# A decoder pair with 32 experts on one core: the order of the experts from sums on TensorE, two experts in fixed order, first loads held, no GpSimd splits in block 2

## The chip, the cores and the metric

The kernel runs on one core of a Trainium2 chip. The time is the device time of one execution in microseconds (us). The engines are TensorE (PE, with its weight loads as PEld), VectorE (DVE), ScalarE (ACT), GpSimd (POOL) and SyncE (SP), which here only issues DMAs and loads registers.

## The reference, cut to what matters

The reference puts two transformer blocks behind one another. The first has two kinds of attention and then a mixture of experts: each token takes 4 of 32 experts by its router logits, and each expert is a pair of float32 matrix products with a gated activation between them. The second block has two more kinds of attention, gates and a plain feed-forward layer. All is float32.

```python
top_val, top_idx = lax.top_k(logits, TOP_K)            # 4 of 32 per token
gates = jax.nn.softmax(top_val, axis=-1)
group_sizes = jnp.bincount(flat_e, length=N_EXPERTS)
hgu = lax.ragged_dot(xs, w_gate_up, group_sizes) + b_gate_up[e_sorted]
act = _clamped_swiglu(hgu)
out = lax.ragged_dot(act, w_down, group_sizes) + b_down[e_sorted]
```

Only the 512 tokens of the sequence reach the output. On the inputs of the reference their 2048 choices fall on the 32 experts as 36, 49, 102, 58, 125, 33, 51, 66, 8, 19, 48, 62, 45, 86, 85, 91, 93, 74, 14, 47, 51, 102, 112, 18, 159, 86, 49, 55, 60, 89, 39, 36 (its routing worked out in float32).

## The kernel before, in words

**Numbers.** A float32 operand is held as two float32r parts, high and low, and a product is three matmuls (high by high and the two cross terms: `mm3`, L364 to L367). So each weight chunk (128 x 2048 values, 1 MB) that SP loads into a raw buffer is split: ACT writes the high part (L192), DVE subtracts it and writes the low part (L194; GpSimd does so for the chunks in `st.on_pool`). There are 7 raw buffers in the expert stage (3, 2 and 2 in three pools, later 8) and 3 pairs of split ones (later 4).

**The stream of chunks.** `Stream` holds all weights of the kernel in the order of their use. `dma()` (L147) issues loads while a raw buffer is free and the number stays below `st.limit`; `split()` splits ahead while a split buffer is free and then calls `dma()`; `get()` hands PE the next chunk and frees the one before; `release()` frees one.

**Experts.** Each expert has 12 chunks in three parts of four: gate (part 0), up (1) and down (2), run in the order (v,0), (v-1,2), (v,1). An expert's tokens are gathered from DRAM by an indirect DMA into `xg` (`rows`, L1414), transposed on PE (`turn_x`), and after the down part scattered with addition (`out`, L1499). A tile of 128 rows ("big") does 12 matmuls per chunk; a tile of 64 rows ("small") puts the high and low part side by side and does 8.

**The order.** The first `FIRST` = 4 experts run in fixed order with big tiles. The other 28 are ranked by the number of their tokens: ranks 0 to 12 get big tiles, rank 0 a small tile more, ranks 13 to 27 small ones. `RANKS` gives the order in which the ranks run: 13, 0, 14, 15, and then big and small by turns. Tokens that don't fit go to overflow tiles, of which rank 0's second is the first; only if there is more than one, a loop behind the experts runs (`n_ov > 1`).

**The routing.** The tables of the first four experts (`table`, `table_out`: the rows to gather, their gates) are made before the expert stage. The rest is the generator `routing()`, of which one step runs after each chunk (`aside`): counts on PE, then on DVE the ranks by comparing all 32 x 32 pairs on all 128 partitions, the order, the overflow bases, each token's rank and slot, the one-hot tiles `rv` (on GpSimd) and `soh`, the table of the other experts on PE, and the experts of the overflow tiles. From the expert `FIRST` on, a load takes its expert's number from a register that SP loads from `ordi`.

**The start of the expert stage** (L1556 on): gather the first rows, release two split buffers (so two splits, each followed by a load on SP), transpose the rows, and then chunk by chunk.

**Block 2.** Its chunks are in the same stream. Those of the q and k projections and the next three, and two of the feed-forward layer, are in `st.on_pool`: 17 splits of the low part on GpSimd. GpSimd also does the power -0.5 of the norms (L362) and the rotations of one attention (L1770 to L1772).

Of the kernel before, what the change touches and what calls it, by code (L numbers as in the profile page):

```python
# [9 lines left out]
F32 = mybir.dt.float32  # L10
# [10 lines left out]
P = 128  # L21
# [18 lines left out]
ALPHA = 2.0 ** 0.25  # L40
NEG = -1e30
# [54 lines left out]
class Stream:  # L96
# [48 lines left out]
    def dma(self, n=1 << 30):  # L145
        while self.n_dma < n:
            key = self._raw_key()  # L147
            if key is None:
                return
            j = self.n_dma  # L150
            a, b = self.shape[j]
            pool, bufs = self.raw_pools[key]
            t = pool.tile([P, CH], F32, tag="raw", bufs=bufs, name="raw")
            s = self.src[j]
            if callable(s):
                s = s()
            d = t[:, :a * b].rearrange("p (a b) -> p a b", a=a)
            if isinstance(s, list):
                w = b // len(s)
                for i, x in enumerate(s):  # L160
                    self.nc.sync.dma_start(out=d[:, :, i * w:(i + 1) * w], in_=x)
            elif j in self.halves:
                for i in range(2):
                    self.nc.sync.dma_start(out=d[:, i * a // 2:(i + 1) * a // 2], in_=s[:, i * a // 2:(i + 1) * a // 2])
# [59 lines left out]
def tile_kernel(ctx: ExitStack, tc: tile.TileContext, a, out, cst):  # L224
# [15 lines left out]
    def bank(name="b"):  # L240
        return ps[0].tile([P, 512], F32, tag="b", bufs=3, name=name)
# [985 lines left out]
    e_ = ExitStack()  # L1227
    pe = open_pool(e_, "pe")
    st.open_raw(3, pe, NRAW)
    st.dma()  # L1230

    def routing():

        def full(name, tag, shape, dtype=BF16):
            return rt.tile([P, *shape], dtype, tag=tag, bufs=1, name=name)

        def down(x, n):
            return x.unsqueeze(2).to_broadcast([P, NE, n])
# [6 lines left out]
        b = bank("cnt")[:, :NE]  # L1245
        for j in range(NT):
            nc.tensor.matmul(b, oneb, asg[:, j], start=j == 0, stop=j == NT - 1)
        ei = iota[:, :NE]
        cnt, key, rank, small_, first = (rt.tile([P, NE], F32, name=n) for n in ("cnt", "key", "rank", "small_", "first"))
        nc.vector.tensor_copy(out=cnt, in_=b)  # L1250

        stt(out=key, in0=cnt, scalar=float(NE), in1=ei, op0=ALU.mult, op1=ALU.subtract)
        ts(out=key[:, :FIRST], in0=ei[:, :FIRST], scalar1=-1.0, scalar2=-BIG, op0=ALU.mult, op1=ALU.add)
        yield
        before = full("before", "A", [NE, NE])
        tt(out=before, in0=across(key, NE), in1=down(key, NE), op=ALU.is_gt)
        red(out=rank, in_=before, axis=AX.X, op=ALU.add)
        yield

        who = full("who", "B", [NE, NE])  # L1260
        order = rt.tile([P, NE], F32, name="order")
        tt(out=who, in0=down(ei, NE), in1=across(rank, NE), op=ALU.is_equal)
        with exact():
            tt(out=who, in0=who, in1=across(ei, NE), op=ALU.mult)
        red(out=order, in_=who, axis=AX.X, op=ALU.add)
        nc.vector.tensor_copy(out=ordi, in_=order[0:1])
        ts(out=sel[:, FIRST:], in0=order, scalar1=pm, scalar2=None, op0=ALU.is_equal)
        yield

        nov, over, base = (rt.tile([P, NE], F32, name=n) for n in ("nov", "over", "base"))  # L1270
        ts(out=first, in0=rank, scalar1=0.0, scalar2=None, op0=ALU.is_equal)
        ts(out=small_, in0=rank, scalar1=float(NB), scalar2=None, op0=ALU.is_ge)
        stt(out=small_, in0=rank, scalar=float(NE - FIRST), in1=small_, op0=ALU.is_lt, op1=ALU.mult)

        stt(out=over, in0=small_, scalar=64.0, in1=cnt, op0=ALU.mult, op1=ALU.add)
        stt(out=over, in0=first, scalar=-64.0, in1=over, op0=ALU.mult, op1=ALU.add)
        nc.vector.tensor_copy(out=nov, in_=first)
        for k in range(4):
            stt(out=nov, in0=over, scalar=129.0 + 128 * k, in1=nov, op0=ALU.is_ge, op1=ALU.add)
        yield  # L1280
        with exact():
            tt(out=before, in0=before, in1=across(nov, NE), op=ALU.mult)
        red(out=base, in_=before, axis=AX.X, op=ALU.add)
# [53 lines left out]
        i_ = iota[:, :NOV].unsqueeze(2).to_broadcast([P, NOV, NE])
        m1, m2 = full("m1", "A", [NOV, NE]), full("m2", "B", [NOV, NE])
        end = rt.tile([P, NE], F32, name="end")
        tt(out=end, in0=base, in1=nov, op=ALU.add)  # L1340
        tt(out=m1, in0=i_, in1=across(base, NOV), op=ALU.is_ge)
        tt(out=m2, in0=i_, in1=across(end, NOV), op=ALU.is_lt)
        yield
        with exact():
            tt(out=m1, in0=m1, in1=m2, op=ALU.mult)
            tt(out=m1, in0=m1, in1=across(ei, NOV), op=ALU.mult)
        red(out=eidf, in_=m1, axis=AX.X, op=ALU.add)
# [219 lines left out]
    hrs, gb2 = [], []

# [580 lines left out]
```

## Time and profile before

| | |
|---|---|
| median of 3 runs | 2328.29 us (2325.48 to 2330.32) |
| the profiled execution | 2326.43 us, its span 2324.3 us |
| mean granted clock of TensorE | 0.969 |
| expert stage in the trace | about 331 to 1496 us |
| block 2 in the trace | about 1499 to 2324 us |

The profile is of one execution. An engine's busy time is what its instructions took; matmuls are pipelined, so 10.0 of 10 us busy means that PE always had one under way. An idle time is put down to the instruction that released the engine.

### The profile page before, as it was taken

How to read it: one execution, taken by the hardware profiler on the slowest of the kernel's cores; microseconds unless marked ns; L12 is line 12 of the kernel's file. 1: busy time of each engine (PE TensorE's matmuls, PEld its weight loads, DVE VectorE, ACT ScalarE, POOL GpSimd, SP SyncE). 2: the span in 40 equal slices, each digit the busy share in tenths (PEclk: the TensorE clock that was granted, in tenths of full speed). 3: DMA queues.
4: the chain of work that ended last, by engine and by line, in shares of the span. 5: the costliest groups of instructions: out<-in, count | busy, mean ns of one | idle time of the engine just before them, and what ended most of it. 6: DMA issues, size and time to landing. Idle time of an engine off the chain costs nothing. (4 is left out here: it accounts for less than half of the span.)

```text
span 2324.3 us, 27360 instructions
## 1 busy us (share of the span) xinstructions
PE 2184.6 (94%) x10215; PEld 1724.1 (74%) x10215; DVE 1660.4 (71%) x1820; ACT 1311.2 (56%) x1407; POOL 400.0 (17%) x299
## 2 busy tenths in 40 slices
PE   7889967999999999999999999789999999999998
PEld 6677855776777777777777777567887888888886
DVE  5875569987598999999999999755565346343435
ACT  3463444776597888888888888534455222232230
POOL 4200031101021101123321232031352003000000
PEclk9999978999999999999999999899999999999999
DMA  6212166998799999999999999742122333222220
GB/s 225 83 49 91 52 224 197 359 355 308 242 367 348 406 394 396 395 396 389 389 391 395 391 391 387 271 120 59 51 73 73 102 134 107 92 92 91 82 100 37
DMA packets 193817, 529.08 MB, mean 228 GB/s; under 512 B 17777, under 2 KB 64761, under 8 KB 193681
## 3 DMA queue, kind: packets, MB, share of 16 engines
q1 hardware_dynamic: 183632, 503.16, 58.5%
q0 software_dynamic: 8320, 19.94, 3.3%
q10 hardware_dynamic: 1728, 4.20, 0.5%
q8 instruction: 82, 1.34, 0.2%
q14 instruction: 55, 0.44, 0.1%
HBM read 510.97 MB, written 25.71 MB: 231 GB/s over the span
## 5 line engine op out<-in xcount | busy, mean ns | idle before, releaser
L194 DVE TENSOR_TENSOR wlo<-raw,whi 128x2048 fp32r<-128x2048 f32 (+2 forms) x439 | 999.8, 2303 | 189.8 <-ACT whi L192 188.8
L192 ACT ACTIVATE whi<-raw 128x2048 fp32r<-128x2048 f32 (+2 forms) x460 | 867.7, 1898 | 348.6 <-PE bk L367 146.2
L1499 POOL DMA_INDIRECT sums_d<-ob,gidx x33 | 96.7, 2932 | 851.2 <-ACT ob L1498 844.8
L366 PE MATMUL gu<-wlo,x 128*128 128x512 f32 x544 | 217.4, 400 | 8.7 <-DVE wlo L194 8.7
L365 PE MATMUL gu<-whi,x 128*128 128x512 f32 x544 | 222.4, 409 | 0.0
L1468 PE MATMUL gu<-wlo,x 128*128 128x512 f32 x512 | 211.2, 412 | 6.1 <-DVE x L371 3.0
L367 PE MATMUL gu<-whi,x 128*128 128x512 f32 x544 | 216.8, 399 | 0.0
L1469 PE MATMUL gu<-whi,x 128*128 128x512 f32 x512 | 204.1, 399 | 0.0
L365 PE MATMUL bk<-xT,wlo 128*128 128x512 f32 (+2 forms) x464 | 187.0, 403 | 0.6 <-ACT xT L370 0.3
L366 PE MATMUL bk<-xT,whi 128*128 128x512 f32 (+2 forms) x464 | 183.1, 395 | 2.1 <-DVE xT L371 2.1
L367 PE MATMUL bk<-xT,whi 128*128 128x512 f32 (+2 forms) x464 | 183.0, 394 | 0.0
L365 PEld LDWEIGHTS gu<-whi,x 128*128 128x128 f32 x544 | 104.3, 192 | 36.3 <-issue 11.4
L366 PEld LDWEIGHTS gu<-wlo,x 128*128 128x128 f32 x544 | 104.1, 191 | 33.3 <-DVE wlo L194 11.3
L1414 POOL DMA_INDIRECT xg<-h_d,gidx x33 | 114.5, 3468 | 77.4 <-PE trx L380 67.6
L194 POOL TENSOR_TENSOR wlo<-raw,whi 128x2048 fp32r<-128x2048 f32 (+2 forms) x21 | 82.6, 3937 | 236.8 <-ACT whi L192 223.1
L367 PEld LDWEIGHTS gu<-whi,x 128*128 128x128 f32 x544 | 103.9, 191 | 23.9
L1468 PEld LDWEIGHTS gu<-wlo,x 128*128 128x128 f32 x512 | 97.9, 191 | 29.4 <-DVE x L371 3.1
L1468 PE MATMUL dn<-wlo,at 128*128 128x512 f32 x256 | 106.7, 417 | 9.7 <-DVE at L371 3.7
L2056 DVE SCALAR_TENSOR_TENSOR xr<-xr,bk 128x512 f32<-128x512 f32 (+1 forms) x42 | 27.8, 661 | 121.4 <-PE bk L367 121.3
L1469 PEld LDWEIGHTS gu<-whi,x 128*128 128x128 f32 x512 | 97.9, 191 | 19.8
L365 PE MATMUL dn<-whi,at 128*128 128x512 f32 x272 | 110.3, 406 | 0.0
L367 PE MATMUL dn<-whi,at 128*128 128x512 f32 x272 | 108.6, 399 | 0.0
(484 smaller groups left out, 4281.4 us busy)
## 6 DMA issues: line engine op xcount, KB each, us to landing
raw<-in_w_gate_up_dram SPq DMA_DIRECT2D x256, 1024.0 KB, 15.7
raw<-in_w_down_dram SPq DMA_DIRECT2D x128, 1024.0 KB, 15.5
raw<-in_w_ff_dram SPq DMA_DIRECT2D x32, 1024.0 KB, 5.6
raw<-in_w_in_dram SPq DMA_DIRECT2D x14, 1024.0 KB, 5.3
raw<-in_w_in_dram SPq DMA_DIRECT2D x24, 256.0 KB, 3.4
raw<-in_w_o_dram SPq DMA_DIRECT2D x4, 1024.0 KB, 5.1
raw<-in_w_in_dram SPq DMA_DIRECT2D x8, 512.0 KB, 7.3
raw<-in_w_out_dram SPq DMA_DIRECT2D x4, 1024.0 KB, 5.0
```

The source lines that it names most:

```text
L192: nc.scalar.activation(out=hi[:, sl], in_=t[:, sl], func=AF.Copy)
L194: eng.tensor_tensor(out=lo[:, sl], in0=t[:, sl], in1=hi[:, sl].bitcast(F32), op=ALU.subtract)
L365: nc.tensor.matmul(o, ll, rh, start=start, stop=False)
L366: nc.tensor.matmul(o, lh, rl, start=False, stop=False)
L367: nc.tensor.matmul(o, lh, rh, start=False, stop=stop)
L1414: nc.gpsimd.indirect_dma_start(out=xg[:self.n], out_offset=None, in_=h1_d, in_offset=bass.IndirectOffsetOnAxis(ap=self.gi[:self.n], axis=0 ...
L1468: nc.tensor.matmul(o, x[0][:, kk], wl[:, k, sl], start=kk == 0, stop=False)
L1469: nc.tensor.matmul(o, x[0][:, kk], wh[:, k, sl], start=False, stop=False)
L1499: nc.gpsimd.indirect_dma_start(out=sums_d, out_offset=bass.IndirectOffsetOnAxis(ap=self.gi[:self.n], axis=0), in_=ob[:self.n], in_offset=N ...
L2056: nc.vector.scalar_tensor_tensor(out=r, in0=r, scalar=ALPHA if first else 1.0, in1=acc[:, sl], op0=ALU.mult, op1=ALU.add)
```

## The change

The routing computes each expert's rank on its own partition (32 partitions, the other 32 experts along the row), and turns what must stand on all partitions into sums over partitions by small matmuls with ones: the order and the ranks in one, the overflow bases in two, the experts of the overflow tiles in one. The one-hot tile `oh` is bfloat16. `FIRST` is 2: two experts run in fixed order, 30 are ranked, and the ranks run as 13, 0, 14, 15, 16, 17, and then big and small by turns, so there are two big tiles fewer and two small ones more. No load is issued from before the first gather until the order stands: the first two steps of the routing run between the two releases and before the first transposes, and then the free raw buffers are filled by loads on ACT's queue. The gather of the third tile waits for the table. No chunk of block 2 is split on GpSimd.

```diff
-FIRST = 4
+FIRST = 2
...
-RANKS = [NB, 0, NB + 1, NB + 2] + [r for i in range(NB - 1) for r in (1 + i, NB + 3 + i)]
-RANKS += list(range(2 * NB + 2, NE - FIRST))
+RANKS = [NB, 0] + list(range(NB + 1, NE - FIRST - NB + 1)) + [r for i in range(NB - 1) for r in (1 + i, NE - FIRST - NB + 1 + i)]
...
-                self.nc.sync.dma_start(out=d, in_=s)
+                self.queue.dma_start(out=d, in_=s)
...
-    st.on_pool.update(range(n2, len(st.src) + 3))
...
-    st.on_pool.update((len(st.src), len(st.src) + 1))
...
-    oh = rt.tile([P, 16, NE], F32, name="oh")
+    oh = rt.tile([P, 16, NE], BF16, name="oh")
...
     st.open_raw(3, pe, NRAW)
-    st.dma()
...
+            nc.tensor.matmul(b[:NE, :NE], oneb[:, :NE], asg[:, j], start=j == 0, stop=j == NT - 1)
+        for j in range(NT):
+            nc.tensor.matmul(b[:NE, NE:NE + 2], asg[:, j], oneb[:, :2], start=j == 0, stop=j == NT - 1)
+        nc.vector.tensor_copy(out=cn, in_=b[:NE, :NE + 2])
+        stt(out=key, in0=cn[:, :NE], scalar=float(NE), in1=ei, op0=ALU.mult, op1=ALU.subtract)
+        ts(out=key[:, :FIRST], in0=ei[:, :FIRST], scalar1=-1.0, scalar2=-BIG, op0=ALU.mult, op1=ALU.add)
+        stt(out=keyp, in0=cntp, scalar=float(NE), in1=me, op0=ALU.mult, op1=ALU.subtract)
+        ts(out=keyp[:FIRST], in0=me[:FIRST], scalar1=-1.0, scalar2=-BIG, op0=ALU.mult, op1=ALU.add)
+        ts(out=mw[:, 0], in0=key, scalar1=keyp, scalar2=None, op0=ALU.is_lt)
+        red(out=rankp_, in_=mw[:, 0], axis=AX.X, op=ALU.add)
+        ts(out=rankp_, in0=rankp_, scalar1=-1.0, scalar2=float(NE - 1), op0=ALU.mult, op1=ALU.add)
+        ts(out=mw[:, 1], in0=ei, scalar1=rankp_, scalar2=me, op0=ALU.is_equal, op1=ALU.mult)
+        nc.tensor.matmul(b[:, :2 * NE], all_, mw.rearrange("p u e -> p (u e)"), start=True, stop=True)
         yield
-        tt(out=before, in0=across(key, NE), in1=down(key, NE), op=ALU.is_gt)
-        red(out=rank, in_=before, axis=AX.X, op=ALU.add)
...
-        tt(out=who, in0=down(ei, NE), in1=across(rank, NE), op=ALU.is_equal)
-            tt(out=who, in0=who, in1=across(ei, NE), op=ALU.mult)
-        red(out=order, in_=who, axis=AX.X, op=ALU.add)
...
+        nc.vector.tensor_copy(out=ordi, in_=b[0:1, NE:2 * NE])
+        ts(out=sel[:, FIRST:], in0=b[:, NE:2 * NE], scalar1=pm, scalar2=None, op0=ALU.is_equal)
+        nc.vector.tensor_copy(out=rows[:, 0], in_=b[:, :NE])
...
+        ts(out=novs[:, :NE], in0=mw[:, 0], scalar1=nov, scalar2=None, op0=ALU.mult)
+        nc.vector.tensor_copy(out=novs[:, NE:], in_=nov.to_broadcast([NE, 2]))
         yield
-            tt(out=before, in0=before, in1=across(nov, NE), op=ALU.mult)
-        red(out=base, in_=before, axis=AX.X, op=ALU.add)
...
+        nc.tensor.matmul(b[:, :NE + 2], all_, novs, start=True, stop=True)
+        nc.tensor.matmul(b[:NE, NE + 2:NE + 4], mw[:, 0], novs[:, NE:], start=True, stop=True)
         yield
+        nc.vector.tensor_copy(out=rows[:, 1], in_=b[:, :NE])
+        nc.vector.tensor_copy(out=eidi[:, NOV:], in_=b[:, NE:NE + 1])
+        nc.vector.tensor_copy(out=basec, in_=b[:NE, NE + 2:NE + 3])
...
         table_out(tb, NC, FIRST)
+        ranked.append(True)
+        next_gather()
         yield
...
+        nc.tensor.matmul(b, all_, m1, start=True, stop=True)
+        yield
+        nc.vector.tensor_copy(out=eidf, in_=b)
...
+    st.limit = st.n_dma
     next_gather()
+    more = routing()
     st.release()
+    next(more)
     st.release()
+    next(more)
     next_turn()
-    more = routing()
+    st.limit, st.queue = n_moe + 2, nc.scalar
+    st.dma()
+    st.queue = nc.sync
```

## Rows read from the trace of the kernel before

**Rows 1.** Page: busy time by engine, and DMA share in 40 slices of 58.1 us.
```profile
PE 2184.6 (94%) x10215; PEld 1724.1 (74%) x10215; DVE 1660.4 (71%) x1820; ACT 1311.2 (56%) x1407; POOL 400.0 (17%) x299
...
DMA  6212166998799999999999999742122333222220
```

**Rows 2.** Stretches: length, each engine's busy us (instructions), granted clock, DMA share, GB/s.
```profile
342.70:417.60 74.90, 62.44 (x243) 46.58 (x241) 67.08 (x89) 35.75 (x26) 10.36 (x5) 0.88 0.62 201
...
492.90:631.50 138.60, 130.48 (x577) 98.58 (x577) 99.64 (x67) 89.20 (x71) 14.67 (x8) 0.98 0.85 296
...
836.00:902.00 66.00, 66.00 (x302) 50.60 (x301) 62.67 (x40) 55.10 (x42) 7.16 (x4) 1.00 1.03 397
...
1540.00:1800.00 260.00, 248.53 (x1386) 205.86 (x1386) 150.66 (x394) 123.28 (x294) 89.60 (x142) 0.98 0.23 70
...
390.00:400.00 10.00, 5.74 (x29) 4.20 (x27) 10.00 (x5) 4.79 (x4) 7.53 (x3) 1.00 0.61 202
...
400.00:410.00 10.00, 9.05 (x28) 7.00 (x29) 9.84 (x14) 1.16 (x1) 0.00 (x0) 0.66 0.82 259
```

**Rows 3.** Waits of PE in the whole span: us in total, times, longest.
```profile
PE trx L380 <- DMA xg<-h_d,gidx: 11.4, 2, 9.8
...
PE gu L366 <- DVE wlo L194: 8.7, 6, 2.6
...
PE tbl L1175 <- POOL rv L1325: 2.2, 1, 2.2
```

**Rows 4.** Timeline of 325 to 345: start us, us, engine, line, operation.
```profile
330.48 6.41 SPq L166 DMA_DIRECT2D raw<-in_w_gate_up_dram  x4
...
331.89 1.15 POOL L1414 DMA_INDIRECT xg<-h_d,gidx  x1 [2.51 <-DVE gidx L1180]
...
340.99 1.97 PE L380 MATMUL trx<-ident,xg 128*128 128x128 f32 x8 [9.80 <-DMA xg<-h_d,gidx]
...
342.77 0.69 DVE L371 TENSOR_TENSOR x<-trx,x 128x512 fp32r<-128x512 f32 x1 [6.27 <-ACT x L370]
```

**Rows 5.** Groups on DVE, 342.7 to 417.6: count | busy us, mean ns | idle before.
```profile
L194 DVE TENSOR_TENSOR wlo<-raw,whi 128x2048 fp32r<-128x2048 f32 x15 | 35.6, 2377 | 2.1 <-ACT whi L192 2.1
...
L1329 DVE TENSOR_TENSOR soh<-cs,slot 128x512 fp32r<-128x512 f32 x4 | 5.3, 1374 | 0.0
...
L1256 DVE TENSOR_TENSOR before<-key 128x1024 bf16<-128x1024 f32 x1 | 1.2, 1218 | 0.0
...
L1341 DVE TENSOR_TENSOR m<-cs,base 128x640 bf16<-128x640 f32 x1 | 0.8, 819 | 0.0
...
L1279 DVE SCALAR_TENSOR_TENSOR nov<-over,nov 128x32 f32<-128x32 f32 x4 | 0.8, 192 | 0.1
```

**Rows 6.** Timeline of PE: where expert parts begin or end.
```profile
417.54 0.72 PE L1457 MATMUL gu<-bstk,sel 64*128 64x512 f32 x2
...
492.82 0.73 PE L1457 MATMUL gu<-bstk,sel 64*128 64x512 f32 x2
...
631.45 0.27 PE L1472 MATMUL dn<-ident 64*64 64x2 f32 x2
...
836.64 0.72 PE L1457 MATMUL gu<-bstk,sel 64*128 64x512 f32 x2
...
902.09 0.72 PE L1457 MATMUL gu<-bstk,sel 64*128 64x512 f32 x2
```

**Rows 7.** Timeline of SP: loads issued, 18 experts apart.
```profile
780.20 20.09 SPq L166 DMA_DIRECT2D raw<-in_w_gate_up_dram  x8
...
1380.18 19.86 SPq L166 DMA_DIRECT2D raw<-in_w_gate_up_dram  x8
```

**Rows 8.** Block 2: GpSimd's splits as a group, then timeline rows of DVE and PE.
```profile
L194 POOL TENSOR_TENSOR wlo<-raw,whi 128x2048 fp32r<-128x2048 f32 (+1 forms) x17 | 70.8, 4167 | 228.6 <-ACT whi L192 214.9 <-DMA braw<-r_d 13.7
...
1948.92 6.79 DVE L194 TENSOR_TENSOR wlo<-raw,whi 128x2048 fp32r<-128x2048 f32 x1
...
1956.37 0.33 PE L366 MATMUL bk<-xT,whi 128*128 128x128 f32 x1 [1.65 <-DVE xT L371]
```

More of the change, by code (lines that the diff above doesn't have):

```diff
@@ L104, in __init__ @@
         self.nc = tc.nc
+        self.queue = tc.nc.sync
         self.src, self.shape = [], []
@@ L160, in dma @@
                 for i, x in enumerate(s):
-                    self.nc.sync.dma_start(out=d[:, :, i * w:(i + 1) * w], in_=x)
+                    self.queue.dma_start(out=d[:, :, i * w:(i + 1) * w], in_=x)
             elif j in self.halves:
                 for i in range(2):
-                    self.nc.sync.dma_start(out=d[:, i * a // 2:(i + 1) * a // 2], in_=s[:, i * a // 2:(i + 1) * a // 2])
+                    self.queue.dma_start(out=d[:, i * a // 2:(i + 1) * a // 2], in_=s[:, i * a // 2:(i + 1) * a // 2])
             else:
-                self.nc.sync.dma_start(out=d, in_=s)
+                self.queue.dma_start(out=d, in_=s)
             self.raw[j] = t
@@ L1244, in routing, with col @@
         exact = lambda: nc.allow_low_precision("small whole numbers")
-        b = bank("cnt")[:, :NE]
+        ei, me, all_ = iota[:NE, :NE], pm[:NE], oneb[:NE]
+        def col(name):
+            return rt.tile([P, 1], F32, name=name)[:NE]
+        b = bank("cnt")
         for j in range(NT):
-            nc.tensor.matmul(b, oneb, asg[:, j], start=j == 0, stop=j == NT - 1)
-        ei = iota[:, :NE]
-        cnt, key, rank, small_, first = (rt.tile([P, NE], F32, name=n) for n in ("cnt", "key", "rank", "small_", "first"))
@@ L1250, in routing @@
-        nc.vector.tensor_copy(out=cnt, in_=b)
-        stt(out=key, in0=cnt, scalar=float(NE), in1=ei, op0=ALU.mult, op1=ALU.subtract)
-        ts(out=key[:, :FIRST], in0=ei[:, :FIRST], scalar1=-1.0, scalar2=-BIG, op0=ALU.mult, op1=ALU.add)
-        yield
-        before = full("before", "A", [NE, NE])
-        tt(out=before, in0=across(key, NE), in1=down(key, NE), op=ALU.is_gt)
-        red(out=rank, in_=before, axis=AX.X, op=ALU.add)
-        yield
-        who = full("who", "B", [NE, NE])
-        order = rt.tile([P, NE], F32, name="order")
@@ L1262, in routing @@
-        tt(out=who, in0=down(ei, NE), in1=across(rank, NE), op=ALU.is_equal)
-        with exact():
-            tt(out=who, in0=who, in1=across(ei, NE), op=ALU.mult)
-        red(out=order, in_=who, axis=AX.X, op=ALU.add)
[L1266 to L1271, printed above, removed]
@@ new lines, in routing @@
+        nc.tensor.matmul(b[:, :2 * NE], all_, mw.rearrange("p u e -> p (u e)"), start=True, stop=True)
+        yield
+        rows = rt.tile([P, 2, NE], BF16, name="rows")
+        nc.vector.tensor_copy(out=ordi, in_=b[0:1, NE:2 * NE])
+        ts(out=sel[:, FIRST:], in0=b[:, NE:2 * NE], scalar1=pm, scalar2=None, op0=ALU.is_equal)
+        nc.vector.tensor_copy(out=rows[:, 0], in_=b[:, :NE])
+        nov, over, first, small_ = (col(n) for n in ("nov", "over", "first", "small_"))
+        ts(out=first, in0=rankp_, scalar1=0.0, scalar2=None, op0=ALU.is_equal)
@@ L1276, in routing @@
+        ts(out=small_, in0=rankp_, scalar1=float(NB), scalar2=None, op0=ALU.is_ge)
+        stt(out=small_, in0=rankp_, scalar=float(NE - FIRST), in1=small_, op0=ALU.is_lt, op1=ALU.mult)
+        stt(out=over, in0=small_, scalar=64.0, in1=cntp, op0=ALU.mult, op1=ALU.add)
         stt(out=over, in0=first, scalar=-64.0, in1=over, op0=ALU.mult, op1=ALU.add)
@@ L1279, in routing @@
             stt(out=nov, in0=over, scalar=129.0 + 128 * k, in1=nov, op0=ALU.is_ge, op1=ALU.add)
+        novs = rt.tile([P, NE + 2], BF16, name="novs")[:NE]
+        ts(out=novs[:, :NE], in0=mw[:, 0], scalar1=nov, scalar2=None, op0=ALU.mult)
+        nc.vector.tensor_copy(out=novs[:, NE:], in_=nov.to_broadcast([NE, 2]))
         yield
-        with exact():
-            tt(out=before, in0=before, in1=across(nov, NE), op=ALU.mult)
-        red(out=base, in_=before, axis=AX.X, op=ALU.add)
-        tot = rt.tile([P, 1], F32, name="tot")
-        red(out=tot, in_=nov, axis=AX.X, op=ALU.add)
-        nc.vector.tensor_copy(out=eidi[:, NOV:], in_=tot)
+        b = bank("bs")
+        nc.tensor.matmul(b[:, :NE + 2], all_, novs, start=True, stop=True)
+        nc.tensor.matmul(b[:NE, NE + 2:NE + 4], mw[:, 0], novs[:, NE:], start=True, stop=True)
         yield
+        basec, end = col("basec"), col("end")
+        nc.vector.tensor_copy(out=rows[:, 1], in_=b[:, :NE])
+        nc.vector.tensor_copy(out=eidi[:, NOV:], in_=b[:, NE:NE + 1])
+        nc.vector.tensor_copy(out=basec, in_=b[:NE, NE + 2:NE + 3])
         of = [rt.tile([P, 16], F32, name=n) for n in ("rankp", "basep")]
-        for x, o in zip((rank, base), of):
+        for x, o in zip((rows[:, 0], rows[:, 1]), of):
             m = full("pairs", "B", [16, NE])
@@ L1334, in routing @@
         table_out(tb, NC, FIRST)
+        assert n_turned[0] == n_gathered[0] == FIRST
+        ranked.append(True)
+        next_gather()
         yield
[L1337 to L1342, printed above, removed]
+        i_ = iota[:NE, :NOV]
+        m1, m2 = (rt.tile([P, NOV], BF16, name=n)[:NE] for n in ("m1", "m2"))
+        tt(out=end, in0=basec, in1=nov, op=ALU.add)
+        ts(out=m1, in0=i_, scalar1=basec, scalar2=me, op0=ALU.is_ge, op1=ALU.mult)
+        ts(out=m2, in0=i_, scalar1=end, scalar2=me, op0=ALU.is_ge, op1=ALU.mult)
+        with exact():
+            tt(out=m1, in0=m1, in1=m2, op=ALU.subtract)
         yield
[L1344 to L1347, printed above, removed]
+        b = bank("eid")[:, :NOV]
+        nc.tensor.matmul(b, all_, m1, start=True, stop=True)
+        yield
+        nc.vector.tensor_copy(out=eidf, in_=b)
         nc.vector.tensor_copy(out=eidi[:, :NOV], in_=eidf)
@@ L1533, in tile_kernel @@
     n_gathered = [0]
+    ranked = []
     def next_gather():
-        if n_gathered[0] < len(tiles):
+        if n_gathered[0] < (len(tiles) if ranked else FIRST):
             tiles[n_gathered[0]].rows()
```

11 lines of the change are left out of this document (5 added, 6 removed).

## The prediction

> **What bounds the kernel now.** I read the page first, then tables of stretches, then the waits of PE, then timelines. On the page PE is busy 94% of the span, and the DMA slices stand at 9 for most of the expert stage [rows 1]. Such a mean joins stages with different limits, so each stage is read by itself [rows 2].
>
> - Start (331 to 343 us): PE waits 9.8 us for the first gather, which competes with four loads of 1 MB issued just ahead of it [rows 3, 4].
> - Routing phase (342.7 to 417.6, the first four expert parts): DVE is busy 67.1 of 74.9 us, PE 62.4, DMA has a share of 0.62 [rows 2]. DVE is the bound: PE waits for its low parts (8.7 us in 6 waits [rows 3]), and raw buffers come free only as fast as DVE splits.
> - The big experts: the stretch 492.9 to 631.5 has PE busy 130.5 of 138.6 us at a DMA share of 0.85 [rows 2]. PE is the bound; loads run into full buffers.
> - The alternating experts (836 to 902): PE busy 66.0 of 66.0, DMA share 1.03 [rows 2]. Both are full; a pair takes 65.45 us on PE [rows 6], and over 18 experts the loads keep a pace of (1380.18-780.20)/18 = 33.33 us per expert [rows 7], that is 66.66 a pair. The loads end last here.
> - Block 2: PE is busy 248.5 of 260 us in 1540 to 1800 [rows 2].
>
> So what is gained before the loads become the bound moves everything behind it; PE work taken out where loads bind is worth nothing.
>
> **The sum, step by step**, against the profiled execution (2326.43 us, span 2324.3; the median of the runs is 1.86 above it).
>
> *Start.* Held loads leave the gather alone. No row shows a gather by itself, so the rows come somewhere between their issue's end (333.0) and 341.0 as now [rows 4]. But the first product needs the low part of the rows, which DVE writes at 342.77 [rows 4], and DVE now has more ahead of it: from 331.9 a split (2.4 [rows 5]), 9 small operations, a split, 15 small ones. A small one is 0.19 [rows 5], so 2.4+1.7+2.4+2.9 = 9.4, to 341.3. Gain 1.5 (bounds 0, and 6 if the small ones cost nothing).
>
> *Loads held.* Four loads start at about 339 instead of from 330.5 on. By the code six chunks are loaded by then (five raw buffers and one that is split). A big part of four chunks takes (492.82-417.54)/6 = 12.55 us on PE [rows 6], 3.1 per chunk, so PE needs the seventh chunk at 342+19 = 361; issued at 339, at 2.8 per chunk (33.33/12 [rows 7]) the first of the four lands near 345 and is split by 350. Cost 0, covered by the six chunks. Without that cover, in a stream that is never idle, it costs 8.5. The four issues on ACT's queue wait for the two splits, which are done by then; ACT is busy 35.8 of 74.9 us in this phase [rows 2], and behind them stands only the next split. SP's register loads wait for the order, which stands at about 339, before the first ranked load at chunk 21. The third gather now waits for the table, 5 to 6 chunks (16 us) ahead of its use; a gather under load took 9.1 (331.89 to 340.99 [rows 4]): hidden.
>
> *Routing on DVE.* Behind the start, these leave DVE: seven operations over 1024 elements at 1.22 = 8.5; four over 640 at 0.82 and one of about 0.5 = 3.8; some 17 small ones at 0.19 = 3.2, most of them moved ahead of the start and counted there [rows 5]. About nine small ones come in (1.7). The bfloat16 `oh` may shorten two products (0 to 0.7; I take 0). Net 15.5-1.7 = 13.8. The four one-hot operations stay (5.3 for four, slowed by `rv` on GpSimd [rows 5]), and so does PE's wait for that (2.2 [rows 3]). DVE then has 67.1-13.8 = 53.3 us, and about 4 idle; PE needs 4 x 12.55 = 50.2 and some 4 for its waits. I take 58 us for the phase instead of 74.8; ends 54 (PE alone) and 66 (half the relief lost, because the new sums wait in PE's order: behind each stand the next chunk's products). It starts 1.5 sooner, so the second expert's up part starts at 399.3 instead of 417.54 [rows 6]: **-18.2**. The added matmuls are a dozen with at most 64 columns, most of them while PE waits for the gather: below 1.
>
> *Two experts, not four.* From there the old stream goes through two big experts (417.54 to 492.82, 75.28 us), and then through the sequence "big, small, rank 0 with two tiles" until 631.45 [rows 6]. The new stream has that sequence at once, and then two small experts more. PE would take 65.45-37.64 = 27.8 for one [rows 6], but with buffers full at the end of rank 0 and four small experts in a row the loads end last: 33.33 each [rows 7], 66.7 for two. **-8.6**; at PE's pace it would be -19.7, and if loads are behind even before, 0.
>
> *Block 2.* 17 splits of 4.17 us leave GpSimd (70.8 [rows 8]) for DVE, at most 17 x 2.4 = 41. DVE suffers from them today: beside one of GpSimd's, a split on DVE took 6.79 instead of 2.4, and PE waited 1.65 for what stood behind it [rows 8]. Two splits in turn on DVE would end 2 us sooner. The Trainium skill says in "SBUF — State Buffer", section "SBUF: two separate sides", that DVE with two operands in SBUF and GpSimd take turns at one port pair by an exclusive lock, so the loser stands still. The 6.79 agrees; by that rule alone DVE would lose nothing at all by the move. The gain can't pass PE's idle time there, 11.5 us [rows 2] and the 1.65; the loss could be 41 if each split came to stand on the path. DVE is busy 150.7 of 260 us [rows 2], with fillers on PE, so I take **-3**.
>
> Sum: -18.2-8.6-3 = -29.8: 2296.6 in the profiled execution, 2298.5 as a median. I predict **2299**.
>
> **The rivals.**
> 1. *The loads keep a lead*, so the small experts run at PE's pace: -18.2-19.7-3 = -40.9, 2287. For it: the DMA share below 1 before 631 [rows 2]. Against: four small experts use up 4 x 5.5 = 22 us of the lead, which is at most ten chunks (28 us), and twelve pairs behind them 1.2 each, so the loads end last all the same.
> 2. *Half the relief is lost*, phase 66 us: -10.2-8.6-3, about 2307. For it: PE's queue is in order and has three new sums in it, and its wait for the table stays [rows 3]. Against: each sum waits for a step that DVE began a chunk earlier.
> 3. *Nothing*: the table or the held loads eat the rest of the gain too, 2324 to 2333.
> 4. *DVE's splits stand in the way in block 2* (slower). Place: 1540 to 1800, where the softmax chain goes through DVE. Price: 2.4 and up to 1.9 of waiting for ACT's high part, 4.3 each. From the seventh of the 17 that lies wholly on the path, the 26.8 of the expert stage are gone; with twelve, 2301.5+52 = 2353. Against: GpSimd's lock holds DVE for 4.2 per split today, and PE still idles only 11.5.
> 5. *The clock falls in the four small experts* (slower). In 400 to 410 the granted clock fell to a mean of 0.66, after PE had been busy 5.7 of 10 us; in those ten it was still 1.00 [rows 2]. At the lower level, 1.2 GHz, a small expert takes up to 55.6 instead of 27.8. The 29.8 are gone if PE runs half of these four experts at that level (27.8+13.9 is 8.4 beyond the loads' 33.3; four times is 33): some 2303 to 2330, at worst 2385. The Trainium skill warns of it in "TensorE: Matmul & The Clock Gate", section "HAM oscillation — how this bites in real kernels": little work between waits for loads lets the clock drop each time. Against: a slow PE leaves no waits behind it, so it would not stay so.
> 6. *The change does not do what it says*: were more than 13 of the 30 ranked experts above 64 tokens, the loop behind the experts would run, an expert with its loads in the open, about 37.6+33.3 more. By the counts, the 14th has 62.
>
> **How the numbers follow.** Forecast 0.52 (its own range 2289 to 2309), rival 1 0.15, rival 2 0.18, rival 3 0.05, rival 4 0.05, rival 5 0.03, rival 6 0.02. The range 2281 to 2317 holds the first three: low end -18.2-19.7-8, high end a phase of 66, the swap at -4 and block 2 at +2. Faster by over 0.2% (4.7 us, about what a measurement of this kernel can tell from no change): 0.86; same 0.05; slower 0.09.
>
> **What would show it.** In the changed profile: rows on PE at about 334 to 338, first product near 342; DVE busy below 58 us from there to the second expert's up part, which starts near 400; rank 0 done near 540; a DMA share of 1 from there to the end of the experts, which comes some 27 us sooner, with PE waiting for loads in experts 4 to 7; in block 2 no DVE operation stretched beside GpSimd. Wrong would be a phase above 66 us, loads late before rank 0, a clock below 1 in the small experts, or more idle time of PE in block 2 than today.

## The result, and the profile after

The changed kernel takes 2293.22 us (median of 4 runs, 2286.52 to 2296.11) against 2327.57 for the kernel before beside it: ratio 0.985, interval 0.982 to 0.987, that is 34.4 us less. Forecast were 2299, between 2281 and 2317. The profiled execution has a span of 2290.9 us; by its rows the experts end 26.3 us sooner (PE's last row of them at 1464.90 instead of 1491.21) and block 2 is 7.1 us shorter. Medians and ratios here and below are of fast executions; one execution of the first run without held loads took 4612.97 us and is not among them.

The page after, busy time by engine and DMA share in 40 slices of 57.3 us:

```profile
PE 2158.6 (94%) x10151; PEld 1699.0 (74%) x10151; DVE 1645.4 (72%) x1837; ACT 1317.7 (58%) x1413; POOL 352.0 (15%) x282
...
DMA  6212158978999999999999999731221233322220
```

PE lost 26 us of work, GpSimd 48. The stretches that answer to [rows 2] (length, PE, PEld, DVE, ACT, POOL busy, granted clock, DMA share, GB/s): routing phase, the sequence with rank 0, the middle of the small experts, a pair, the attention of block 2, and of the routing phase its start and all that comes from the first low part on.

```profile
337.10:403.70 66.60, 59.55 (x241) 45.02 (x240) 56.75 (x83) 35.76 (x25) 11.04 (x5) 0.90 0.83 278
403.70:539.80 136.10, 128.63 (x577) 97.39 (x576) 99.61 (x67) 89.14 (x71) 14.96 (x8) 0.99 0.88 313
577.90:638.40 60.50, 57.19 (x261) 40.54 (x261) 60.36 (x39) 57.52 (x45) 23.96 (x4) 1.00 1.03 398
834.00:900.00 66.00, 66.00 (x300) 50.43 (x298) 62.67 (x40) 55.58 (x42) 7.14 (x4) 1.00 1.03 397
1513.60:1773.60 260.00, 249.61 (x1387) 207.43 (x1386) 151.79 (x407) 123.74 (x294) 35.78 (x128) 0.98 0.22 66
...
337.10:345.10 8.00, 6.48 (x18) 4.41 (x18) 3.04 (x17) 0.84 (x2) 1.02 (x1) 0.57 0.80 236
339.14:403.68 64.54, 58.29 (x237) 44.50 (x237) 54.97 (x70) 35.16 (x24) 10.02 (x4) 0.91 0.85 285
```

What the reader is to see: the routing phase fell from 74.9 to 66.6 us, and from the first low part on, as the prediction counts it, from 74.8 to 64.5, not to 58; its DMA share rose from 0.62 to 0.83. In the middle of the small experts DVE is busy all the time and PE at the full clock. The pairs and the attention look as before.

The start, answering to [rows 4]: gather, transposes and first low part (start us, us, engine, line, operation):

```profile
330.77 1.16 POOL L1425 DMA_INDIRECT xg<-h_d,gidx  x1 [2.54 <-DVE gidx L1178]
...
335.25 1.94 PE L378 MATMUL trx<-ident,xg 128*128 128x128 f32 x8
...
339.14 1.27 DVE L369 TENSOR_TENSOR x<-trx,x 128x512 fp32r<-128x512 f32 x2
```

The transposes come 4.5 us behind the gather's issue instead of 9.1, the low part 8.37 instead of 10.88. PE began them right behind the first of the new sums, so the rows may have been there sooner. The issue itself lies at 330.77 instead of 331.89, which proves little: over the profiled executions it lies between 327.79 and 333.64, with the same code ahead of it in most.

PE's landmarks, answering to [rows 6]: the second expert's up part, the end of rank 0, one pair apart, and the last row of the experts.

```profile
403.68 0.72 PE L1468 MATMUL gu<-bstk,sel 64*128 64x512 f32 x2
...
539.82 0.27 PE L1483 MATMUL dn<-ident 64*64 64x2 f32 x2
...
834.04 0.72 PE L1468 MATMUL dn<-bstk,sel 64*128 64x512 f32 x2
...
899.48 0.72 PE L1468 MATMUL dn<-bstk,sel 64*128 64x512 f32 x2
...
1464.90 0.27 PE L1483 MATMUL dn<-ident 64*64 64x2 f32 x2
```

So the shift is -13.9 at the second expert's up part (417.54 before), and rank 0 is done at 539.82 (631.45 before, with two big experts more ahead of it). A pair is 65.44 long, as before (65.45).

One place gave some of it back: block 2's constants, which `aside` starts behind expert 8. First come SP's queue there (their eight small loads, and the weights behind them), the DMA's rate, and ACT's wait for the late weights:

```profile
684.75 2.30 SPq L1365 DMA_DIRECT2D posi<-in_positions_dram  x1
687.16 4.67 SPq L1368 DMA_DIRECT2D work<-in_lambda_q_dram  x1
...
700.94 0.54 SPq L1373 DMA_DIRECT2D work<-in_rel_bias_dram  x1
702.55 2.45 SPq L166 DMA_DIRECT2D raw<-in_w_gate_up_dram  x4
```

```profile
689.00:699.00 10.00, 10.00 (x45) 7.86 (x44) 9.26 (x8) 9.46 (x8) 0.00 (x0) 1.00 0.95 371
699.00:709.00 10.00, 10.00 (x50) 7.53 (x48) 7.00 (x5) 4.41 (x4) 4.49 (x3) 1.00 0.74 166
709.00:719.00 10.00, 5.35 (x15) 3.95 (x15) 5.78 (x4) 5.97 (x5) 0.27 (x1) 0.68 1.04 341
```

```profile
709.71 1.91 ACT L192 ACTIVATE whi<-raw 128x2048 fp32r<-128x2048 f32 x1 [5.78 <-DMA raw<-in_w_gate_up_dram]
```

Then come PE's two long waits in this pair of experts, and, ahead of the second, some of the work on the constants on ACT (the load of a function table) and the DMA's rate beside it:

```profile
PE gu L363 <- DVE x L369: 4.7, 1, 4.7
PE dn L1492 <- ACT bstk L1487: 2.8, 1, 2.8
```

```profile
741.52 1.28 ACT L1402 ACT_TABLE_LOAD   x1
```

```profile
744.00:749.00 5.00, 3.13 (x14) 2.25 (x12) 3.34 (x8) 4.39 (x5) 0.00 (x0) 1.00 1.02 408
```

For 18 us no weights are issued, the rate falls to 166 GB/s, and right behind it PE is busy 5.35 of 10 us at a clock of 0.68. The pair with this stall takes 81.3 us (PE's rows 709.22 to 790.53) instead of 65.4; in the kernel before it took 74.4 (740.62 to 815.00). Of the 15.9 us, 8.8 fall in its first part, behind the late weights (709.22 to 739.64, 30.4 us instead of the 21.6 of other pairs), and 7.1 in its second, beside the work that DVE and ACT do on the constants; there the loads run on at 408 GB/s. The prediction did not see this place.

### The profile page after: what moved, and what is told of

It reads as the page before. It is cut to its first block, busy times and chain, and to the rows that moved or that the text cites. A ratio compares the mean times of both kernels' runs of the same rounds, so it can differ in the third digit from the quotient of the medians.

```text
span 2290.9 us, 27281 instructions
## 1 busy us (share of the span) xinstructions
PE 2158.6 (94%) x10151; PEld 1699.0 (74%) x10151; DVE 1645.4 (72%) x1837; ACT 1317.7 (58%) x1413; POOL 352.0 (15%) x282
## 5 line engine op out<-in xcount | busy, mean ns | idle before, releaser
L194 DVE TENSOR_TENSOR wlo<-raw,whi 128x2048 fp32r<-128x2048 f32 (+2 forms) x456 | 1029.5, 2283 | 215.9 <-ACT whi L192 213.7
L1480 PE MATMUL gu<-whi,x 128*128 128x512 f32 x576 | 227.6, 395 | 0.0
L363 PE MATMUL gu<-whi,x 128*128 128x512 f32 x480 | 198.0, 413 | 6.2 <-DVE x L369 6.2
L365 PE MATMUL gu<-whi,x 128*128 128x512 f32 x480 | 192.2, 400 | 0.0
L1425 POOL DMA_INDIRECT xg<-h_d,gidx x33 | 131.5, 3985 | 52.7 <-PE trx L378 34.6
L1479 PE MATMUL dn<-wlo,at 128*128 128x512 f32 x288 | 120.1, 417 | 9.8 <-DVE wlo L194 3.5
L1480 PEld LDWEIGHTS gu<-whi,x 128*128 128x128 f32 x576 | 109.0, 189 | 21.7
L363 PEld LDWEIGHTS gu<-whi,x 128*128 128x128 f32 x480 | 92.5, 193 | 38.9 <-issue 9.7
L360 POOL TENSOR_TENSOR bnrs<-bnrs,mhalf 128x1 f32<-128x1 f32 (+1 forms) x21 | 29.3, 1398 | 577.0 <-DVE bnrs L398 577.0
L1480 PE MATMUL dn<-whi,at 128*128 128x512 f32 x288 | 114.2, 396 | 0.0
L2075 DVE SCALAR_TENSOR_TENSOR xr<-xr,bk 128x512 f32<-128x512 f32 (+1 forms) x42 | 27.8, 662 | 118.8 <-PE bk L365 118.8
L365 PEld LDWEIGHTS gu<-whi,x 128*128 128x128 f32 x480 | 92.3, 192 | 21.7
L363 PE MATMUL bk<-whi,fT 128*128 128x512 f32 (+1 forms) x272 | 103.8, 382 | 0.5 <-DVE xr L2075 0.5
```

The source lines that it names most:

```text
L194: eng.tensor_tensor(out=lo[:, sl], in0=t[:, sl], in1=hi[:, sl].bitcast(F32), op=ALU.subtract)
L360: nc.gpsimd.tensor_tensor(out=dst, in0=dst, in1=mhalf[:n, :w], op=ALU.pow)
L363: nc.tensor.matmul(o, ll, rh, start=start, stop=False)
L365: nc.tensor.matmul(o, lh, rh, start=False, stop=stop)
L1425: nc.gpsimd.indirect_dma_start(out=xg[:self.n], out_offset=None, in_=h1_d, in_offset=bass.IndirectOffsetOnAxis(ap=self.gi[:self.n], axis=0 ...
L1479: nc.tensor.matmul(o, x[0][:, kk], wl[:, k, sl], start=kk == 0, stop=False)
```

## The experiments

All had the kernel before beside them on the same chip, and the ratios are to it; its medians were 2326.83 (runs 1 to 4), 2329.52 (the first run of 5, and 6, 7 and 8) and 2327.80 (the second run of 5, the changed kernel again, and 9 and 10). Differences to the changed kernel are to its median of 2293.22, where no other is named.

**1. Constants early.**

```diff
-            if v > 8:
+            if v > 2:
                 next(consts2, 0)
```

> The changed kernel with one edit: the eight small loads of block 2's constants run beside expert 3 (rank 0), where the buffers are full, instead of beside expert 9. Theory A (from the four small experts on, the end of the experts is set by the loads, and what stops the load queue there delays all behind it): in 689 to 709 the changed kernel moved 371 and 166 GB/s instead of 410, which is 6.9 us of load time; these come back, so about 2286, experts' end near 1458, and the pair behind the constants takes less than its present 81 us. Rival B (PE sets the pace of the pairs, and the stall beside expert 9 is only lead that was used up by the small experts): the stall comes anyway, 2291 to 2295. Rival C: the constants cost as much beside rank 0, 2293 or more.

Measured: 2287.01 (2286.28 to 2289.77), ratio 0.9835 (0.9821 to 0.9848); experts' end 1459.93 instead of 1464.90. The window of the constants in the new place, and the pair that had stalled:

```profile
455.00:468.00 13.00, 12.81 (x55) 10.45 (x56) 5.40 (x4) 5.26 (x3) 0.00 (x0) 1.00 0.79 260
...
710.60:778.00 67.40, 66.26 (x299) 49.95 (x298) 61.99 (x39) 55.60 (x42) 17.10 (x5) 1.00 1.03 396
```

Beside rank 0 the same loads cost PE 0.2 us. Theory A holds; the pair takes 67.3 us now (PE's rows 710.63 to 777.97), near the loads' 66.66 of [rows 7]. The edit moves the work done on the constants too, but in the changed kernel the loads ran on beside that work. What was lost is the load time: from this pair's start to the experts' end it takes 749.3 us instead of 755.7, 6.4 less, of the 6.9 that were expected. That the loads come late through the pairs of this run is seen in ACT's waits for them (710.6 to 1460):

```profile
ACT whi L192 <- DMA raw<-in_w_down_dram: 68.3, 60, 2.2
```

**2 and 3. GpSimd's splits again: all 17, or only the two of the feed-forward layer.**

```diff
 # 2
+    st.on_pool.update(range(n2, len(st.src) + 3))
 # 2 and 3
+    st.on_pool.update((len(st.src), len(st.src) + 1))
```

> The changed kernel with all 17 splits of block 2 on GpSimd again. Theory A (the 7.1 us that block 2 became shorter are one stall of 1.65 us and the low clock behind it, both beside a split on GpSimd just before the feed-forward layer; the other 15 cost about what they bring): 2299 to 2301. Rival B (the gain in block 2 belongs to the state that the experts leave it in, not to the splits): 2292 to 2295. The prediction's own term for it was 3 us: 2296.

> The changed kernel with only the two splits of the feed-forward layer on GpSimd again, the 15 of the attention on VectorE. Theory A (the stall and the clock behind it, see the run with all 17): as that run within 2 us, so 2298 to 2301, with a granted clock near 0.6 in some 10 us before the feed-forward layer. Rival B (the 15 in the attention bring it): 2293 to 2295.

Measured: 2299.15 (ratio 0.988, 0.9865 to 0.9896) and 2300.54 (0.989, 0.9875 to 0.9905). Two splits do what 17 do: theory A in both. The timeline of run 3, just ahead of the feed-forward layer:

```profile
1923.21 4.61 POOL L194 TENSOR_TENSOR wlo<-raw,whi 128x2048 fp32r<-128x2048 f32 x1
...
1923.22 6.76 DVE L194 TENSOR_TENSOR wlo<-raw,whi 128x2048 fp32r<-128x2048 f32 x1
...
1930.63 0.33 PE L365 MATMUL bk<-xT,whi 128*128 128x128 f32 x1 [1.63 <-DVE xT L370]
```

And the two stretches behind it:

```profile
1930.00:1940.00 10.00, 9.37 (x49) 9.27 (x50) 2.56 (x5) 1.82 (x3) 0.00 (x0) 0.62 0.51 192
1940.00:1950.00 10.00, 10.00 (x39) 7.97 (x38) 5.05 (x5) 3.66 (x4) 0.00 (x0) 0.87 0.31 107
```

The same place in the changed kernel has two splits on DVE in turn (timeline), and no fall of the clock behind them (stretch):

```profile
1922.09 4.49 DVE L194 TENSOR_TENSOR wlo<-raw,whi 128x2048 fp32r<-128x2048 f32 x2
```

```profile
1929.00:1939.00 10.00, 10.00 (x63) 8.90 (x63) 4.79 (x5) 4.42 (x6) 0.00 (x0) 1.00 0.26 97
```

A wait of 1.63 us, and the clock fell to a mean of 0.62 over 10 us (3.8 us lost) and 0.87 over the next (1.3): 6.7 us together, near the 7.3 that the two splits cost. Run 2 and the kernel before show the same wait (1.65 us) and a clock of 0.60 and 0.57 over the 10 us behind it. The 15 splits in the attention are worth nothing that these intervals show. There DVE's load is the thing to see, in run 2 (15 on GpSimd) and in the changed kernel, 1513.6 to 1773.6, the groups of the softmax's scaling and of DVE's own splits (mean ns behind the busy time):

```profile
L1861 DVE TENSOR_SCALAR e<-e,den 128x128 f32<-128x128 f32 (+3 forms) x48 | 42.2, 879 | 1.1
...
L194 DVE TENSOR_TENSOR wlo<-raw,whi 128x2048 fp32r<-128x2048 f32 x2 | 4.5, 2288 | 4.4 <-ACT whi L192 4.4
```

```profile
L194 DVE TENSOR_TENSOR wlo<-raw,whi 128x2048 fp32r<-128x2048 f32 (+1 forms) x17 | 34.5, 2041 | 34.0 <-ACT whi L192 32.9 <-DMA raw<-in_w_in_dram 1.1
...
L1859 DVE TENSOR_SCALAR e<-e,den 128x128 f32<-128x128 f32 (+3 forms) x48 | 18.6, 387 | 1.1
```

Beside GpSimd's splits 48 operations that don't even split anything took 23.6 us more; so DVE took over 15 splits, 30.0 us (4.5 to 34.5), and its busy time there grew by 3.7 only (148.1 to 151.8).

**4. The swap undone.**

```diff
-FIRST = 2
+FIRST = 4
...
+RANKS = [NB, 0, NB + 1, NB + 2] + [r for i in range(NB - 1) for r in (1 + i, NB + 3 + i)]
...
-        next_gather()
```

> The changed kernel with four experts in fixed order again, and the ranks run as 13, 0, 14, 15 and then big and small by turns. Theory A (two big experts cost 75.3 us, the two small ones in their place 60.6 as they ran, and about 7 of these 14.7 us are given back where the loads have no lead, beside the constants of block 2): 8 us slower than the changed kernel, about 2301; the record's term was 8.6. Rival B (the small experts' 30.3 us each stay, nothing is given back): 14.7 slower, 2308. Rival C (the loads bind all through, the swap is worth nothing): 2293.

Measured: 2303.80 (2301.80 to 2305.66), ratio 0.9907 (0.9892 to 0.9922). The end of the experts in its trace:

```profile
1477.15 0.27 PE L1482 MATMUL dn<-ident 64*64 64x2 f32 x2
```

Counted from the gather's issue (332.70 here, 330.77 in the changed kernel) the experts end 1144.5 us later, and 1134.1 in the changed kernel: 10.3 us; the time is 10.6 longer. The pair with the constants took 74.3 us here (PE's rows 727.08 to 801.37) and 81.3 in the changed kernel: of what the swap brought, 7 us were given back there. Theory A is nearest; its 8 us were 2 too low.

**5. Loads not held**, run twice.

```diff
     st.open_raw(3, pe, NRAW)
+    st.dma()
...
-    st.limit = st.n_dma
...
-    st.limit, st.queue = n_moe + 2, nc.scalar
-    st.dma()
-    st.queue = nc.sync
+    st.limit = n_moe + 2
```

> The changed kernel with the loads not held: four loads of 1 MB go out before the first gather, as in the kernel before, and none on ScalarE's queue. Theory A (the held loads only free the gather; six chunks cover their lateness): the first rows land about 4 us later, the first product starts 2.6 to 4 us later, and all behind it too: 2296 to 2297. Rival B (the four loads are missed: the stream is never idle behind them): faster by up to 8.5, 2285 to 2290. Rival C (neither shows at the end): 2292 to 2294.

> Loads not held, once more, beside the changed kernel. The run before came out 7 to 8 us slower, of which its trace shows 2.4 from the first gather (10.8 instead of 8.4 us from its issue to the first low part of the rows) and 2.9 from work ahead of the gather that is the same in both. Theory A (held loads are worth the 2.4 and what follows from it; the rest was the place of that run): 2 to 4 us slower than the changed kernel. Rival B (the whole belongs to the held loads, through the DMA queues ahead of the gather too): 6 to 9 us slower, with the gather issued near 333.5 again instead of 330.7 to 332.

> The changed kernel itself, as the measure for the other three on the same chip: 2290 to 2296.

Measured: 2299.96 in the first run (2298.16 to 2302.26; ratio 0.988, 0.9859 to 0.99); in the second 2297.82 (2294.71 to 2298.09), with the changed kernel beside it at 2294.01 (2291.48 to 2296.64); ratios 0.9867 (0.985 to 0.9884) and 0.9853 (0.9839 to 0.9868). So without held loads the kernel is slower by 6.7 us in the first run and by 3.8 in the second, there with overlapping intervals; over both, 8 executions have a mean of 2298.6, and 9 of the changed kernel one of 2293.4. The second run's gather and transposes:

```profile
331.27 1.16 POOL L1426 DMA_INDIRECT xg<-h_d,gidx  x1 [2.54 <-DVE gidx L1178]
...
340.76 1.94 PE L378 MATMUL trx<-ident,xg 128*128 128x128 f32 x8 [5.09 <-DMA xg<-h_d,gidx]
```

9.5 us from the issue to the transposes, 4.5 with the loads held; the first low part came at 342.51 (11.2 behind the issue, against 8.37). Nothing is lost by the lateness of the held loads: from the first low part to the second expert's up part it took 65.2 and 66.0 us in these two runs, and 64.5 and 65.6 in the two profiles of the changed kernel. Counted from the gather's issue, the experts end 1139.5 us later in the second run, 1137.7 in the first, and 1134.1 and 1134.6 in the two profiles of the changed kernel: 3 to 5 us, of which 2.4 to 2.9 are the gather's. So rival B falls in the second run, and rivals B and C of the first record with it: nothing is gained by the early loads. Theory A holds in the second run. The first run's time is some 3 us above its theory A; in its profiled execution (2298.16) the gather was issued at 333.64, 2.9 later than in the changed kernel's first profile.

**6 and 7. `rv` on VectorE; the table one chunk later.**

```diff
 # 6
-            nc.gpsimd.tensor_tensor(out=rv[:, :, j], in0=voh, ...
+            tt(out=rv[:, :, j], in0=voh, ...
 # 7
+        yield
         tb = xbank("tbl2")
```

> The changed kernel with the three products `rv` on VectorE instead of GpSimd. Beside them VectorE's own operations are 3.0 us longer in the changed kernel (two `soh` 2.87 for 1.28, a split 3.67 for 2.28), and on VectorE the three would take 3.0 (the same shape as `voh`, 1.02 each). Theory A (VectorE is the bound of the routing phase, so it is a wash): 2291 to 2295, VectorE's busy time in the phase near 57. Rival B (PE's wait of 2.2 us for `rv` and the low clock behind it, 0.67 in 10 us, are what the phase lost against the record's 58 us): 2286 to 2289, phase near 62.

> The changed kernel with the table's matmuls one chunk later, so that PE has the products of one more chunk while GpSimd and VectorE make `rv` and `soh`. Theory A (PE's two waits of 2.2 and 1.6 us at the table, and the clock of 0.67 in the 10 us behind them, 3.3 us, are a loss of their own): phase near 60 instead of 66.6, 2286 to 2289. Rival B (VectorE was busy all of these 10 us and is the bound, PE then waits for low parts instead): 2291 to 2294.

Measured: 2292.27 (ratio 0.9841, 0.9823 to 0.9858) and 2293.71 (0.9842, 0.9823 to 0.9861): no change at the end, theory A of run 6 and rival B of run 7. In the run with the later table, PE's longest group of waits, and the stretch of the table:

```profile
PE gu L364 <- DVE wlo L194: 5.0, 3, 3.2
```

```profile
365.00:375.00 10.00, 5.95 (x25) 3.90 (x23) 10.00 (x7) 5.28 (x5) 7.54 (x3) 1.00 0.52 207
```

The waits for `rv` and `soh` are gone, and PE waits nearly as long for low parts (5.0 us, where it waited 1.7 for them and 3.8 for the table); DVE is busy 10.0 of 10 us. DVE is the bound there. The phase itself did become shorter, 62.7 and 62.1 us from the first low part on instead of 64.5 and 65.6, but not the experts: the sequence with rank 0 took 137.6 and 137.7 us instead of 136.1, and the experts end 1134.8 and 1134.6 us behind the gather's issue, where the two profiles of the changed kernel have 1134.1 and 1134.6. With `rv` on DVE the four `soh` fell from 1075 to 680 ns each, but three products of about 1.0 us came in.

**8 and 9. Edits together.** Constants early and the table later; and `rv` on VectorE too.

> Both: the constants' loads beside expert 3, and the table one chunk later. Theory A (the loads set the end of the experts, and both edits move the loads sooner; gains add up): the run with the early constants gave 6 us, so 2287 less what the later table brings by itself: 2280 to 2283 if that is 4 to 7, 2287 if it is nothing. Rival B (what is gained in the routing phase is given back while the buffers are full, in rank 0's stretch): 2287 whatever the table brings.

> Constants early, table one chunk later, and `rv` on VectorE: the version that should be fastest. Theory A (VectorE is the bound of the routing phase, `rv` there is a wash): 2284 to 2287, as without the last edit. Rival B (GpSimd's three products, now beside PE's products, still cost VectorE 3 us that its own would not): 2281 to 2283.

Measured: 2285.62 (2284.12 to 2286.52), ratio 0.9814 (0.9797 to 0.9831), and 2285.49 (2284.80 to 2289.83), ratio 0.9825 (0.981 to 0.984). These are the fastest versions, some 8 us below the changed kernel, of which 6 are the constants; what the other two edits bring is within the spread (run 1 gave 2287.01 without them). That is rival B of run 8, and theory A only for a later table that brings nothing; in run 9 theory A holds.

**10. The kernel before, constants early.**

```diff
-            if v > 8:
+            if v > 4:
                 next(consts2, 0)
```

> The kernel before with one edit: the constants' small loads beside its rank 0 (expert 5) instead of beside expert 9. Its trace shows 205 and 354 GB/s instead of 410 in the 20 us of these loads, 6.4 us of load time. Theory A (the loads set the end of the experts in the kernel before as well): 6 us faster than before, 2319 to 2323. Rival B (before still had a lead there that hides them): 2325 to 2329.

Measured: 2320.44 (2316.71 to 2326.54), ratio 0.9970 (0.9958 to 0.9982): 7.4 us. The two pairs behind its rank 0, the second of which had stalled:

```profile
675.00:740.00 65.00, 65.00 (x296) 49.75 (x295) 62.41 (x41) 55.42 (x42) 14.69 (x5) 1.00 1.03 397
740.00:806.00 66.00, 66.00 (x300) 50.62 (x299) 62.65 (x40) 55.60 (x43) 7.15 (x4) 1.00 1.03 395
```

PE never waits in them. From the second of them (738.01) to the experts' end (1482.34) it takes 744.3 us, 6.3 less than before (740.62 to 1491.21), of 6.4 expected. Theory A holds in both kernels: behind rank 0, load time that is lost is lost at the end.

## Why the prediction was right, point by point

- *Start*, forecast -1.5: from the gather's issue to the first low part 10.88 became 8.37, so **-2.5**; the 15 small operations ahead of it on DVE took 2.1 us, not 2.9 (0.13 to 0.23 us each, most of them on 32 partitions). That the low part waits for DVE, and not for the gather, was right: PE's first product waits 1.52 us for it. Another 1.1 is the place of this execution's gather.
- *Loads held*, forecast 0: **0**, by run 5 (65.2 and 66.0 us behind the first low part without, 64.5 and 65.6 with).
- *Routing on DVE*, forecast a phase of 58 us: from the first low part to the second expert's up part it was 64.5 instead of 74.8, so **-10.2** in place of -16.8. This is the step that failed, and nearly the time of rival 2 (66). It failed in "DVE then has 53.3 us, and about 4 idle". DVE had 54.97 in these 64.54 us, near the forecast: its other work fell by 16.4 us, more than the 13.8 expected, but 16 splits instead of 14 fell into the phase (37.8 us instead of 33.4). What was wrong is the idle time: 9.6 us, 8.7 of it in three waits for ACT's high parts. The longest of these is at the start; the rows behind it show what GpSimd's `rv` costs DVE (3.0 us: 2.87 and 3.67 instead of 1.28 and 2.28), which the forecast held as it was before:

```profile
346.81 2.29 DVE L194 TENSOR_TENSOR wlo<-raw,whi 128x2048 fp32r<-128x2048 f32 x1 [6.39 <-ACT whi L192]
...
363.98 3.56 POOL L1332 TENSOR_TENSOR rv<-voh,cs 128x832 fp32r<-128x832 bf16 x1 [25.48 <-DVE voh L1330]
...
367.21 2.87 DVE L1336 TENSOR_TENSOR soh<-cs,slot 128x512 fp32r<-128x512 f32 x2
369.99 3.67 DVE L194 TENSOR_TENSOR wlo<-raw,whi 128x2048 fp32r<-128x2048 f32 x1
```

  ACT's split at the start waited 7.03 us for PE: all three split pairs were full until PE had done its first chunk, at a clock of 0.57 in these 8 us. So DVE stood idle for 6.4 us, just when it had been relieved, and was the bound again 20 us later. This is read from the trace; no run had a fourth pair. No run undoes the routing's edits alone either. But with the swap undone (65.2), without held loads (65.2 and 66.0) and with the splits back (63.9 and 64.7) the phase stays near 64.5, so its 10 us are not theirs. Rival 2 named another reason (the new sums wait in PE's order); behind the start none of PE's main waits is on them, and runs 6 and 7 show that the wait for the table was not it either.
- *Two experts, not four*, forecast -8.6: **-10.0** at the experts' end (26.3 less the start's 3.6, the 10.2, and 2.5 by which the sequence with rank 0 became shorter, 136.1 instead of 138.6, which no term held); 10.3 by run 4. The 2.5 stand in the rows: a wait of PE for a gather there is 0.9 us instead of 1.6, and the clock behind it stays up (the kernel before, then the changed one, 40 us behind the sequence's start). The mechanism was right, the size off twice: the small experts ran at 30.3 us (PE's rows 572.05, 602.39 and 632.70), between PE's 27.8 and the loads' 33.33, since DVE bound them (60.36 of 60.5 us) while a lead was left; and 7 us of that went at the constants, of which 2 came back along the pairs.

```profile
532.80:542.80 10.00, 9.22 (x38) 6.80 (x39) 7.48 (x4) 7.00 (x6) 2.98 (x2) 0.83 1.02 354
```

```profile
443.70:453.70 10.00, 9.29 (x44) 6.50 (x44) 9.16 (x5) 8.01 (x8) 3.06 (x2) 1.00 1.03 351
```

- *Block 2*, forecast -3: **-7.1**. The row of the 1.65 us wait was in [rows 8]; its price was taken as 1.65, and the clock behind it (5.1 us lost in the 20 us shown here of the kernel before) was left out. That the 15 others cost nothing was right.

```profile
1950.00:1960.00 10.00, 8.35 (x54) 8.11 (x53) 6.91 (x3) 1.08 (x2) 3.55 (x1) 0.89 0.73 255
1960.00:1970.00 10.00, 10.00 (x41) 9.06 (x41) 3.54 (x5) 4.26 (x5) 0.00 (x0) 0.60 0.09 32
```

  The Trainium skill, "SBUF — State Buffer", section "SBUF: two separate sides", has it that an operation of DVE in a mode with two ports, or with two operands from SBUF, and GpSimd hold the shared ports by turns, and the loser stands still. The trace agrees for the split: 6.76 beside one of 4.61 is that and 2.2 for its own. `e<-e,den` has one operand from SBUF and still fell from 879 to 387 ns; by the page it would have to run in the mode with two ports, which no row shows.
- The sum: -2.5 - 1.1 - 10.2 - 2.5 - 10.0 - 7.1 = -33.4, as the spans differ (2324.3 and 2290.9). One term was 6.6 too large; the start, the swap and block 2 were 1.0, 1.4 and 4.1 too small, and 3.6 came that no term held. So the errors cancel, and that the total came within 6 us of the forecast is in part luck.
- *Rivals.* Rival 1 (the lead stays) fell: behind the stall three pairs take 65.45 us, PE's pace, and from 986.89 to the end they take 66.5 to 67.7, the loads' pace; in run 1 all pairs do (66.5 to 68.6). Rival 2 came near in time, for another reason. Rivals 3 and 6 would have cost time that isn't there. Rival 4 fell, DVE grew by 3.7 us. Rival 5 fell: the clock's mean is 1.00 in the last three small experts and 0.94 in the first (540 to 571), behind a wait of 2.94 us for DVE. It fell further, to 0.68, at the stall that the constants made, a place that no rival named. The Trainium skill, "TensorE: Matmul & The Clock Gate", section "HAM oscillation — how this bites in real kernels", tells of a kernel whose clock fell at every wait for loads. That case did not arise here: through the pairs of run 1 the loads bind, but PE's waits are 1.6 us at most, and the clock's mean is 1.00 from 640 to 1460.

Open: why the first run without held loads took 2299.96, why the gather beside rank 0 came sooner, whether a fourth split pair would have brought the rest of the routing's relief, and what moves the gather's issue by up to 6 us between executions with nearly the same code ahead.

## What to carry to other kernels

Where loads end last, whatever else sits in their queue is paid almost in full: put small transfers where the buffers are full. Price a short wait of PE with the low clock that can follow it, which ahead of the feed-forward layer cost three times the wait. And an engine that is relieved ahead of a stage gains only as much as the buffers let it work ahead.

## What was not expected of the hardware

- Eight small loads, by the code some 0.2 MB together, held SP's queue for 13 to 18 us and cost 6.4 to 6.9 us of load time (166 and 371 GB/s in two stretches of 10 us, instead of 410).
- Behind a wait of 1.63 to 1.65 us the clock had a mean of 0.57 to 0.60 over the next 10 us, that is mostly its lower level, 1.2 GHz, in each of the three traces that have the two splits on GpSimd (the kernel before, runs 2 and 3). But not every such wait is followed by a fall: behind 1.88 us in the changed kernel it stayed at 1.00.

```profile
454.87 0.50 PE L1479 MATMUL gu<-wlo,x 128*128 128x512 f32 x1 [1.88 <-DVE l L1503]
```

```profile
454.87:464.87 10.00, 10.00 (x43) 8.19 (x44) 4.25 (x3) 3.83 (x2) 0.00 (x0) 1.00 0.97 369
```

- A DVE operation with one operand from SBUF beside a value per partition (`e<-e,den`, up to 512 values) took 2.3 times as long on average beside GpSimd's splits (879 and 387 ns).
- With no weights' loads issued ahead of it, the first gather took at most 4.5 us from its issue to the transposes; with four loads of 1 MB ahead it took 9.0 to 9.5.
